# The last layer norm of a hybrid MoE step: taken without the last unit's rows, over two engines

## The chip, the cores and the metric

The kernel runs on one core of a Trainium2 chip, in one launch. The metric is the device time of that launch in microseconds (us). The kernel before took 878.97, 879.23 and 880.75 us in three runs, a median of 879.23. PE is the matrix engine, DVE the vector engine, ACT the scalar engine, POOL the general-purpose engine, which also issues the transfers of the software queue q0, and SP the engine that issues those of the hardware queue q1.

## The reference, cut to what matters

One layer over 512 prompt tokens and 64 sample tokens, 576 rows of D = 1024 float32. An input projection feeds sparse attention and a causal convolution; both are merged, projected and normed to `x1`. Then each token goes through two of 16 experts, and the second norm gives the result:

```python
h2 = x1 * (1 + sc2) + sh2
x  = layer_norm(ALPHA * x1 + (1 + g2) * hier_moe(h2, ...), ln2_g, ln2_b)
# layer_norm: (x - mean) / sqrt(var + 1e-5) * g + b, over the 1024 columns
# returns y_prompt (512 x 1024), y_sample (64 x 1024), and the new caches
```

## The kernel before, in words

Tokens lie in five tiles: four of 128 rows and one of 64. The program is written in the order of the data flow, and a scheduler of the tile framework sets each engine's own order and its waits.

**The front part.** After the conditioning vectors have been computed, three fills on POOL (L416, L418) write a constant row over and over to DRAM: one to the upper half of `z_scr`, and one for the prompt and one for the sample tokens to `h_scr`. Their sources are rows in `rows_scr`, which short POOL transfers (L412) have written just before. Then comes the input projection. For the indexer's keys, `kip` and `kis` are built on ACT and DVE, and POOL writes them out (L504). The indexer's queries come from five groups of matmuls (`tm0` to `tm4`, L144 to L146), whose results ACT copies to the tiles `st` (L514). `kis` and the `st` tiles 0, 2 and 4 share two buffers (the tag "S"), so the copy of tile 2 takes the buffer of `kis`, after `kis` has been written out.

**The MoE stage.** The scratch array `z_scr` has two halves of 576 rows, which add up to ALPHA * x1 before the experts. A token's first choice adds to its row in the lower half, its second choice to its row in the upper half. Thirteen units of work run one after the other; each takes up to 128 gathered token rows through one expert (or 64 through each of two) and ends in `add_rows`: two products on DVE (L1193), then one indirect transfer on POOL that adds the 128 rows to `z_scr` (L1194); rows that are not taken have an index out of bounds and are skipped. The last unit holds one expert. Expert weights go through a ring of 24 pieces of 128 x 1024 floats, loaded by SP.

**The end.** After the last unit, every engine reads the number of experts that had more tokens than their rows (`ovi`, L1492) and runs a loop over them, which is empty with these inputs. Then SP loads each tile's two halves of `z_scr` as one transfer (`zt`, L1525, 1 MB for a full tile). DVE adds the halves (L1527) and multiplies by the gain and adds the bias in two passes (L1529, L1530), with the mean and the root from ACT (for the first tile from DVE), and SP stores the tile to the result (L1531).

## Time and profile before

| | |
|---|---|
| runs, median | 878.97, 879.23, 880.75 us; 879.23 us |
| profiled execution | 880.75 us |
| its span on the core | 879.1 us |
| busy PE / DVE / ACT / POOL | 792.4 / 647.6 / 358.5 / 132.3 us |
| moved by q1 (SP) / q0 (POOL) | 122.74 MB / 34.26 MB |
| chain that ended last: PE / DVE / DMA / issue | 60% / 7% / 4% / 2% |

The span runs from the first to the last recorded event; the execution's own time is 1.65 us longer than it. The chain of waits is followed back from the last instruction, at each step to what released it. "DVEq", "SPq" and the like are an engine's own queue work (reading a value, issuing a transfer). In a timeline a bracket holds the idle time ahead of the instruction and what ended it.

### The profile page before, as it was taken

Reading aid. Unit: us, or ns where it says so; the run is one execution under the profiler, and the core shown is the slowest. Engines: PE = TensorE matmul, PEld = TensorE weight load, DVE = VectorE, ACT = ScalarE, POOL = GpSimd, SP = SyncE. Lnnn points to the kernel's source line nnn. Section 1 sums busy time; section 2 is a strip of 40 time slices with the busy share of each in tenths; the row PEclk is TensorE's granted clock in tenths of the full one; section 3 lists DMA queues with packets and bytes.
Section 4 is the critical chain, followed back from the end, with each engine's and each line's share of the span. In section 5 each row is a group of like instructions: output and inputs, shape, how many; then the busy total and the mean of one; then the engine's idle time right before and its main releaser. Section 6 shows DMA issues by size and latency. Waiting matters only on the chain.

```text
span 879.1 us, 13265 instructions
## 1 busy us (share of the span) xinstructions
PE 792.4 (90%) x4827; PEld 641.6 (73%) x4827; DVE 647.6 (74%) x1275; ACT 358.5 (41%) x654; POOL 132.3 (15%) x169
## 2 busy tenths in 40 slices
PE   4899999999999999999999999899938999999910
PEld 3788888887878879879899799888826676645400
DVE  1569999989999889988896425428896896655337
ACT  3243141324344335547733852312433664334304
POOL 2300000310100000000100001020347342221100
PEclk9999999999999999999999999899957999999965
DMA  9998663482423224232443106585695999699345
GB/s 295 343 340 261 195 213 119 122 241 54 149 71 95 76 75 113 89 100 84 129 118 113 39 1 228 188 259 213 197 329 139 345 366 310 199 363 373 97 164 169
DMA packets 101202, 162.06 MB, mean 184 GB/s; under 512 B 9667, under 2 KB 67163, under 8 KB 101137
## 3 DMA queue, kind: packets, MB, share of 16 engines
q1 hardware_dynamic: 87104, 122.74, 42.3%
q0 software_dynamic: 12688, 34.26, 14.5%
q10 hardware_dynamic: 1344, 4.22, 1.3%
q8 instruction: 38, 0.62, 0.3%
q14 instruction: 28, 0.22, 0.1%
HBM read 146.01 MB, written 26.13 MB: 196 GB/s over the span
## 4 chain that ended last, share of the span: by engine, by line
PE 60%; DVE 7%; DMA 4%; issue 2%; ACT 1%; POOL 1%; POOLq 0%; DVEq 0%; ACTq 0%
PE acc L242 7%; PE acc L244 7%; PE acc L243 7%; PE pd L1182 5%; PE pdot L528 3%; PE pg L1152 2%; PE pg L144 2%; DMA wraw<-in_w_att_out_dram 2%; PE pg L146 2%; PE pg L145 2%; PE tm L144 2%; PE tm L146 2%; PE tm L145 2%; PE pl L652 2%; PE po L660 2%
## 5 line engine op out<-in xcount | busy, mean ns | idle before, releaser
L588 DVE SCALAR_TENSOR_TENSOR y<-ue,dwT,y 128x604 f32<-128x604 f32 (+17 forms) x232 | 183.3, 828 | 1.9 <-ACT y L586 1.6
L242 PE MATMUL acc<-hh,wlo 128*128 128x288 f32 (+1 forms) x504 | 152.9, 304 | 1.3 <-DVE wlo L140 1.3
L243 PE MATMUL acc<-hh,whi 128*128 128x288 f32 (+1 forms) x504 | 150.6, 299 | 0.0
L244 PE MATMUL acc<-hl,whi 128*128 128x288 f32 (+1 forms) x504 | 149.4, 300 | 0.0
L139 ACT CAST whi<-wraw 128x1024 fp32r<-128x1024 f32 (+1 forms) x72 | 75.1, 1044 | 175.2 <-PE acc L244 83.1
L140 DVE TENSOR_TENSOR wlo<-wraw,whi 128x1024 fp32r<-128x1024 f32 (+1 forms) x72 | 87.4, 1214 | 53.6 <-ACT whi L139 53.3
L242 PEld LDWEIGHTS acc<-hh,wlo 128*128 128x128 f32 (+1 forms) x504 | 94.4, 187 | 17.2 <-issue 8.8
L243 PEld LDWEIGHTS acc<-hh,whi 128*128 128x128 f32 (+1 forms) x504 | 94.4, 187 | 5.2 <-issue 5.1
L244 PEld LDWEIGHTS acc<-hl,whi 128*128 128x128 f32 (+1 forms) x504 | 93.7, 187 | 5.5 <-issue 5.2
L144 PE MATMUL tm<-wlo,hh 128*128 128x512 f32 x128 | 50.5, 397 | 0.4 <-DVE wlo L140 0.4
L145 PE MATMUL tm<-whi,hh 128*128 128x512 f32 x128 | 50.4, 394 | 0.0
L146 PE MATMUL tm<-whi,hl 128*128 128x512 f32 x128 | 49.8, 391 | 0.0
L140 DVE TENSOR_TENSOR wlo<-ring,whi 128x1024 fp32r<-128x1024 f32 x30 | 36.4, 1222 | 17.7 <-ACT whi L139 15.0
L1182 PE MATMUL pd<-ring,hT 128*128 128x512 f32 x96 | 44.0, 601 | 1.2 <-ACT hT L1166 1.2
L139 ACT CAST whi<-ring 128x1024 fp32r<-128x1024 f32 x30 | 31.3, 1048 | 31.2 <-PE pg L146 27.4
L242 PE MATMUL acc<-oh,wlo 128*128 128x288 f32 x128 | 39.7, 310 | 4.5 <-DVE gt L744 4.0
L244 PE MATMUL acc<-yl,whi 128*128 128x288 f32 x128 | 39.3, 310 | 0.6 <-DVE yl L721 0.5
L244 PE MATMUL acc<-ol,whi 128*128 128x288 f32 x128 | 39.3, 310 | 0.0
L243 PE MATMUL acc<-oh,whi 128*128 128x288 f32 x128 | 39.2, 307 | 0.0
L243 PE MATMUL acc<-yh,whi 128*128 128x288 f32 x128 | 38.3, 301 | 0.0
L242 PE MATMUL acc<-yh,wlo 128*128 128x288 f32 x128 | 37.9, 297 | 0.0
L1194 POOL DMA_INDIRECT z_scr<-yo,idt x13 | 22.3, 1712 | 83.2 <-DVE yo L1193 74.4
(482 smaller groups left out, 1773.5 us busy)
## 6 DMA issues: line engine op xcount, KB each, us to landing
ring<-in_w_gate_up_dram SPq DMA_DIRECT2D x62, 512.0 KB
wraw<-in_w_in_dram SPq DMA_DIRECT2D x48, 512.0 KB
wada<-in_w_ada_dram SPq DMA_DIRECT2D x32, 512.0 KB
ring<-in_w_down_dram SPq DMA_DIRECT2D x32, 512.0 KB
wada<-in_w_ada_dram SPq DMA_DIRECT2D x32, 256.0 KB
gates_scr<-glg POOLq DMA_DIRECT2D x16, 288.0 KB
gt<-gates_scr POOLq DMA_DIRECT2D x16, 288.0 KB
wraw<-in_w_conv_out_dram SPq DMA_DIRECT2D x8, 512.0 KB
```

The lines of the kernel that those rows point to most:

```text
L139: split_copy[0] = S.copy(hi, raw).ins
L140: V.tensor_tensor(lo, raw, hi, op=OP.subtract)
L144: PE.matmul(out, lh, rl, start=start, stop=False)
L145: PE.matmul(out, lh, rh, start=False, stop=False)
L146: PE.matmul(out, ll, rh, start=False, stop=stop)
L242: PE.matmul(ps[h][0:m, 0:288], wl[:, k, :], xh[:, k, sl], start=k == 0, stop=False)
L243: PE.matmul(ps[h][0:m, 0:288], wh[:, k, :], xh[:, k, sl], start=False, stop=False)
L244: return PE.matmul(ps[h][0:m, 0:288], wh[:, k, :], xl[:, k, sl], start=False, stop=k == KT - 1).ins
L528: PE.matmul(pdt[0:n, 0:L], qiT[pr, h // 2, 128 * t:128 * t + n], kiT[pr, k0:k0 + L], start=True, stop=True)
L588: V.scalar_tensor_tensor(y[:, 30 - i:EXT], ue[:, 0:EXT - 30 + i], dwT[:, j, i:i + 1], y[:, 30 - i:EXT], op0=OP.mult, op1=OP.add)
L1182: PE.matmul(pd_[c], hT[:, k, :], dns[0][k][:, cs], start=k == 0, stop=k == 1)
L1194: sc = G.indirect_dma_start(out=z_d, out_offset=bass.IndirectOffsetOnAxis(ap=ids[1], axis=0), in_=y, in_offset=None, bounds_check=2 * T - ...
```

## The change

The result arrays are filled with the bias row `ln2_b` early, right behind the fills of `h_scr` (L421 of the changed kernel, 512 and 64 rows of 4 KB). At the end, `z_scr` is loaded into free ring pieces once the last but one unit's scatter has landed, so without what the last unit adds, and the five tiles are normed from it: DVE adds the halves and takes the sum of each row in the same pass, ACT squares and takes the root, ACT scales, DVE multiplies by the gain, and POOL adds the tile to the filled result. The last unit's tokens go apart: POOL gathers their rows of both halves of `z_scr`, DVE adds the unit's product, and this sixth tile is normed in full and written over the result by two indirect transfers (prompt rows, sample rows), behind the stores of the five tiles. The last unit's scatter to `z_scr` stays, for the overflow loop, which now has a norm of its own in its body; the loop's count is read at the very end.

```diff
--- before.py
+++ after.py
@@ -413,9 +413,12 @@
         if j >= 2:
             G.dma_start(dap(rows_d, 8 * D + c, [[D, 2], [1, 512]]), bR[32 * j:32 * j + 1, :, :])
 
-    G.dma_start(dap(z_d, T * D, [[D, T], [1, D]]), dap(rows_d, 9 * D, [[0, T], [1, D]]))
+    zero = G.dma_start(dap(z_d, T * D, [[D, T], [1, D]]), dap(rows_d, 9 * D, [[0, T], [1, D]]))
     for s, (t0, n) in enumerate(((0, SEQ), (SEQ, DEC))):
-        G.dma_start(dap(h2_d, t0 * D, [[D, n], [1, D]]), dap(rows_d, (6 + s) * D, [[0, n], [1, D]]))
+        zero = G.dma_start(dap(h2_d, t0 * D, [[D, n], [1, D]]), dap(rows_d, (6 + s) * D, [[0, n], [1, D]]))
+    with tc.issue_after(zero.ins):
+        for s, n in enumerate((SEQ, DEC)):
+            G.dma_start(dap(o["y"][s], 0, [[D, n], [1, D]]), dap(a["ln2_b"], 0, [[0, n], [1, D]]))
 
...
@@ -1272,6 +1275,16 @@
...
+    other = late.tile([128, NE], I32, name="other", bufs=1)
+    sample = late.tile([128, NE], I32, name="sample", bufs=1)
+
+    def other_rows():
+        V.scalar_tensor_tensor(tok, idt[:, 0], 2.0, idt[:, 1], op0=OP.mult, op1=OP.subtract)
+        V.tensor_scalar(other, tok, float(T), None, op0=OP.add)
+        V.tensor_scalar(tok, idt[:, 0], float(SEQ), float(OOB), op0=OP.is_lt, op1=OP.mult)
+        V.scalar_tensor_tensor(sample, idt[:, 0], -float(SEQ), tok, op0=OP.add, op1=OP.add)
+
     def static_args(es):
         e = es[0]
         w = wsl[:, e:e + 1] if e < NFIX else cols[:, 1, e - NFIX:e - NFIX + 1]
@@ -1298,6 +1311,78 @@
...
+    NR2 = NT + 1
+    st2 = late.tile([128, 4, NR2], F32, name="st2", bufs=1)
+    V.memset(st2, 1.0)
+
+    def both_rows(t):
+        return [[(16, 0), (16, 1)], [(16, 2), (16, 3)], [(17, 0), (18, 0)], [(17, 1), (18, 1)], [(17, 2), (18, 2)],
+                [(17, 3), (18, 3)]][t]
+
+    z12, last_rows = {}, [None, None]
+
+    def tile_rows(t):
+        z12[t] = [piece(*x)[0:TS[t]] for x in both_rows(t)]
+        for i, z in enumerate(z12[t]):
+            last_rows[0] = SY.dma_start(z, dap(z_d, (i * T + t * 128) * D, [[D, TS[t]], [1, D]])).ins
+
+    def z_gather(dst, idx):
+        last_rows[1] = G.indirect_dma_start(out=dst, out_offset=None, in_=z_d,
+                                            in_offset=bass.IndirectOffsetOnAxis(ap=idx, axis=0),
+                                            bounds_check=2 * T - 1, oob_is_err=False).ins
+
+    def unit_rows():
+        z12[NT] = [piece(*x) for x in both_rows(NT)]
+        z_gather(z12[NT][1], other[:, plan[-1][0]:plan[-1][0] + 1])
+        z_gather(z12[NT][0], idt[:, 1, plan[-1][0]:plan[-1][0] + 1])
+
+    def summed(t, to=None):
+        z, n = z12[t][0], z12[t][0].shape[0]
+        V.scalar_tensor_tensor(z, z, 1.0, z12[t][1] if to is None else to, op0=OP.mult, op1=OP.add,
+                               accum_out=st2[0:n, 0, t:t + 1])
+        V.tensor_scalar(st2[0:n, 0, t:t + 1], st2[0:n, 0, t:t + 1], -1.0 / D, None, op0=OP.mult)
+
+    def measured(t):
+        z, jk = z12[t]
+        n = z.shape[0]
+        S.activation(jk, z, AF.Square, bias=st2[0:n, 0, t:t + 1], accum_out=st2[0:n, 1, t:t + 1])
+
+    def rooted(t):
+        S.activation(st2[:, 2, t:t + 1], st2[:, 1, t:t + 1], AF.Sqrt, bias=epst, scale=1.0 / D)
+
+    def scaled(t):
+        V.reciprocal(st2[:, 2, t:t + 1], st2[:, 2, t:t + 1])
+        if t < NT:
+            z, n = z12[t][0], TS[t]
+            V.tensor_tensor(st2[:, 3, t:t + 1], st2[:, 0, t:t + 1], st2[:, 2, t:t + 1], op=OP.mult)
+            S.activation(z, z, AF.Identity, bias=st2[0:n, 3, t:t + 1], scale=st2[0:n, 2, t:t + 1])
+
+    rows3 = []
+
+    def rows3_loads():
+        rows3.extend(piece(16, 4 + i) for i in range(2))
+        brow(rows3[0], a["ln2_g"], 0, SY)
+        brow(rows3[1], a["ln2_b"], 0, SY)
+
+    def tile_done(t):
+        z, n = z12[t][0], TS[t]
+        V.tensor_tensor(z, z, rows3[0][0:n], op=OP.mult)
+        with tc.issue_after(last_rows[1]):
+            G.dma_start(dap(o["y"][t // 4], (t % 4) * 128 * D, [[D, n], [1, D]]), z, accum_op=OP.add)
+
+    def unit_done():
+        z, t = z12[NT][0], NT
+        V.scalar_tensor_tensor(z, z, st2[:, 0, t:t + 1], rows3[0], op0=OP.add, op1=OP.mult)
+        V.scalar_tensor_tensor(z, z, st2[:, 2, t:t + 1], rows3[1], op0=OP.mult, op1=OP.add)
+
+    def unit_store():
+        z, e = z12[NT][0], plan[-1][0]
+        for s, (idx, n) in enumerate(((idt[:, 0, e:e + 1], SEQ), (sample[:, e:e + 1], DEC))):
+            G.indirect_dma_start(out=dap(o["y"][s], 0, [[D, n], [1, D]]), out_offset=bass.IndirectOffsetOnAxis(ap=idx, axis=0),
+                                 in_=z, in_offset=None, bounds_check=n - 1, oob_is_err=False)
+
...
@@ -1380,6 +1465,14 @@
         rows_in(0)
         pend, over = [], overflow()
 
+        def do(fn, *args):
+            return lambda: fn(*args)
+
+
+        aside = {("p", len(units) - 3): [rows3_loads],
+                 ("p", len(units) - 2): [do(tile_rows, t) for t in range(2)] + [unit_rows] +
+                                        [do(tile_rows, t) for t in range(2, NT)]}
+
         def product(p):
             p.y = gate_row(p.ar[2], p.ar[3])
             p.pd = down(p.hT, p.dns)
@@ -1388,6 +1481,8 @@
                 if y.left == 0:
                     follow_down(y)
             add_rows(p.y, p.pd, p.ar[0])
+            for act in aside.pop(("p", p.u), ()):
+                act()
 
         for u, x in enumerate(units):
             if u == 2:
@@ -1399,11 +1494,12 @@
                     if len(y.es) == 2:
                         y.blocks[0] = (y.blocks[0][0], static_args(y.es))
                 token_columns(cols[:, 0, NFULL:NVAR], NFIX + NFULL, NE)
+                other_rows()
             owed[0] = int(u + 1 < len(units) and len(units[u + 1].es) == 2)
             blocks = []
             for b, _ in x.blocks:
                 p = Unit()
-                p.b, p.experts = b, x.experts
+                p.b, p.u, p.experts = b, u, x.experts
                 p.ar = dict(x.blocks)[b]
                 p.dns = [y.down for y in x.experts]
                 blocks.append(p)
@@ -1482,12 +1578,25 @@
                 step(2, q)
                 step(3, q)
             pend = blocks
-        rows3 = slot([128, 2, D], name="rows3")
-        brow(rows3[:, 0], a["ln2_g"], 0, SY)
-        brow(rows3[:, 1], a["ln2_b"], 0, SY)
-        for i in range(len(pend)):
-            turn_next(i)
-            product_next(i)
+        p = pend[0]
+        turn_next(0)
+        p.y = gate_row(p.ar[2], p.ar[3])
+        p.pd = down(p.hT, p.dns)
+        add_rows(p.y, p.pd, p.ar[0])
+        for t in range(NT + 2):
+            if t == 1:
+                V.tensor_tensor(z12[NT][0], z12[NT][0], z12[NT][1], op=OP.add)
+            if t < NR2:
+                summed(t, p.y if t == NT else None)
+                measured(t)
+            if t > 1:
+                tile_done(t - 2)
+            if t > 0:
+                scaled(t - 1)
+            if t < NR2:
+                rooted(t)
+        unit_done()
+        unit_store()
 
...
-    jk = slot([128, D], name="jk")
-
-    def act_stats(src, n):
-        mv = late.tile([128, 4], F32, name="mv", tag="mv", bufs=NT)
-        S.activation(jk[0:n], src[0:n], AF.Copy, scale=1.0 / D, accum_out=mv[0:n, 0:1])
-        V.tensor_scalar(mv[0:n, 3:4], mv[0:n, 0:1], -1.0, None, op0=OP.mult)
-        S.activation(jk[0:n], src[0:n], AF.Square, bias=mv[0:n, 3:4], accum_out=mv[0:n, 1:2])
-        S.activation(mv[0:n, 2:3], mv[0:n, 1:2], AF.Sqrt, bias=epst[0:n], scale=1.0 / D)
-        V.reciprocal(mv[0:n, 2:3], mv[0:n, 2:3])
-        return mv[0:n, 0:1], mv[0:n, 2:3]
-
-    for t in range(NT):
-        n, s = TS[t], int(t == 4)
-        z2 = slot([128, 2, D], name="zt")
-        SY.dma_start(z2[0:n], dap(z_d, t * 128 * D, [[D, n], [T * D, 2], [1, D]]))
-        zt = z2[:, 0, :]
-        V.tensor_tensor(zt[0:n], zt[0:n], z2[0:n, 1, :], op=OP.add)
-        mean, rs = stats(zt, n) if t == 0 else act_stats(zt, n)
-        V.scalar_tensor_tensor(zt[0:n], zt[0:n], mean, rows3[0:n, 0], op0=OP.subtract, op1=OP.mult)
-        V.scalar_tensor_tensor(zt[0:n], zt[0:n], rs, rows3[0:n, 1], op0=OP.mult, op1=OP.add)
-        SY.dma_start(dap(o["y"][s], (t % 4) * 128 * D, [[D, n], [1, D]]), zt[0:n])
+        ln2 = slot([128, 2, D], name="ln2")
...
```

The first place is POOL's program in the front part, between the fills and the attention's first outputs. Before:

```order
L412 DMA rows_scr<-arow 2x512 x4
L440 DMA ckt<-in_cache_k_dram 128x256
L442 DMA ckt<-in_cache_idx_k_dram 128x64 x2
L418 DMA h_scr<-rows_scr 512x1024
L418 DMA h_scr<-rows_scr 64x1024
L504 DMA out_dram<-kip 128x4x64
L504 DMA out_dram<-kis 64x64
L559 DMA out_dram<-at_1572 128x256 x3
```

And of the changed kernel:

```order
L412 DMA rows_scr<-arow 2x512 x4
L443 DMA ckt<-in_cache_k_dram 128x256
L445 DMA ckt<-in_cache_idx_k_dram 128x64 x2
L418 DMA h_scr<-rows_scr 512x1024
L418 DMA h_scr<-rows_scr 64x1024
L421 DMA out_dram<-in_ln_b_dram 512x1024
L421 DMA out_dram<-in_ln_b_dram 64x1024
L507 DMA out_dram<-kip 128x4x64
L507 DMA out_dram<-kis 64x64
L562 DMA out_dram<-at_1574 128x256 x3
```

The fill of the result, 576 rows of 4 KB, now stands ahead of the two transfers that write `kip` and `kis`; nothing else moved here.

The second place is ACT's program around the copies of the indexer's queries. Before:

```order
L514 COPY st_1825<-tm0_1684 128x512
L503 COPY kip_1653<-kip_1653 128x4x64
L514 COPY st_1839<-tm1_1685 128x512
L514 COPY st_1867<-tm3_1687 128x512
L139 CAST whi_1970<-wraw_1968 128x1024
L503 COPY kis_1654<-kis_1654 64x64
L508 COPY at2_1572<-pki_1665 128x512
L581 COPY ue_2730<-yT_587 128x512
L582 COPY ue_2730<-stT_97 128x30
...
L508 COPY at2_1572<-pki_1681 128x64
L514 COPY st_1853<-tm2_1686 128x512
L519 COPY at2_1572<-pqi_1833 128x4x128
```

And of the changed kernel:

```order
L517 COPY st_1841<-tm1_1687 128x512
L517 COPY st_1869<-tm3_1689 128x512
L506 COPY kis_1656<-kis_1656 64x64
L511 COPY at2_1574<-pki_1667 128x512
L584 COPY ue_2732<-yT_587 128x512
...
L139 CAST whi_1972<-wraw_1970 128x1024
...
L511 COPY at2_1574<-pki_1683 128x64
L517 COPY st_1855<-tm2_1688 128x512
L522 COPY at2_1574<-pqi_1835 128x4x128
```

A weight cast (`whi`) moved behind the copy of `kis`; the copy of tile 2 (`st_1853<-tm2_1686`, now `st_1855<-tm2_1688`) stays behind it and still takes the buffer that `kis` had, so in both it waits for the transfer that writes `kis` out.

The third place is the end of POOL's program, from the gather of the last unit's rows on. Before, where the last unit's scatter stands behind the overflow loop (whose body is left out):

```order
L1119 DMA xg<-h_scr,idt 128x1024
L1194 DMA z_scr<-yo,idt 1152x1024 x5
L1492 TENSOR_LOAD ovi
L1494 COMPARE_AND_BRANCH
...
L1194 DMA z_scr<-yo,idt 1152x1024
L1572 UNCONDITIONAL_BRANCH
```

And of the changed kernel, down to the loop's count (the last unit's scatter is the single one behind the first store to `out_dram`):

```order
L1122 DMA xg<-h_scr,idt 128x1024
L1197 DMA z_scr<-yo,idt 1152x1024 x5
L1332 DMA ring<-z_scr,other 128x1024
L1332 DMA ring<-z_scr,idt 128x1024
L1373 DMA out_dram<-ring 128x1024
L1197 DMA z_scr<-yo,idt 1152x1024
L1373 DMA out_dram<-ring 128x1024 x3
L1373 DMA out_dram<-ring 64x1024
L1383 DMA out_dram<-ring,idt 512x1024
L1383 DMA out_dram<-ring,sample 64x1024
L1601 TENSOR_LOAD ovi
L1603 COMPARE_AND_BRANCH
```

The five stores, which SP issued behind the loop before, are now POOL's; in the same queue stand two gathers ahead of them, the last unit's scatter behind the first of them, and two scatters behind the last. The count is read behind all of these.

## Rows read from the trace of the kernel before

**Rows 1.** Chain of waits, last 41 us: start us, us, what it waited on or did.
```profile
838.95 0.56 DVEq L1492
...
840.92 6.11 DMA z_scr<-yo,idt
847.05 5.42 DMA zt<-z_scr
852.49 1.24 DVE zt L1527
...
873.71 1.28 DVE zt L1530
```

**Rows 2.** Timeline of the last stretch: start us, us, engine, line, operation [idle before <-releaser].
```profile
830.54 1.55 POOL L1194 DMA_INDIRECT z_scr<-yo,idt  x1 [9.11 <-DVE yo L1193]
...
838.16 0.69 DVE L1193 TENSOR_TENSOR yo<-yo,pd 128x512 f32<-128x512 f32 x1 [0.63 <-PE pd L1182]
...
859.16 16.39 SPq L1531 DMA_DIRECT2D out_dram<-zt  x5
```

**Rows 3.** Windows: stretch, us, busy us (instructions) of five engines, PEclk, DMA share, GB/s.
```profile
832.50:835.50 3.00, 1.52 (x5) 0.81 (x6) 0.54 (x2) 1.80 (x3) 0.00 (x0) 1.00 0.55 75
835.50:841.00 5.50, 2.62 (x7) 0.83 (x5) 2.60 (x3) 0.89 (x1) 0.08 (x1) 1.00 0.00 0
843.00:847.00 4.00, 0.00 (x0) 0.00 (x0) 0.00 (x0) 0.00 (x0) 0.00 (x0) 0.50 0.43 64
852.50:859.20 6.70, 0.00 (x0) 0.00 (x0) 6.55 (x9) 1.45 (x3) 0.00 (x0) 0.50 1.04 414
620.30:624.70 4.40, 4.40 (x27) 3.75 (x25) 4.23 (x9) 2.32 (x4) 0.92 (x1) 1.00 0.70 112
```

**Rows 4.** Groups by shape of DVE and ACT, 839 to 879: xcount | busy us, mean ns | idle before.
```profile
L1529 DVE SCALAR_TENSOR_TENSOR zt<-zt,mv,rows 128x1024 f32<-128x1024 f32 x4 | 5.1, 1284 | 1.6 <-ACT jk L1517 1.5
...
L1527 DVE TENSOR_TENSOR zt<-zt 128x1024 f32<-128x1024 f32 x4 | 4.9, 1216 | 13.6 <-DMA zt<-z_scr 13.6
...
L1519 DVE RECIPROCAL mv<-mv 128x1 f32<-128x1 f32 x3 | 0.5, 155 | 0.0
...
L1517 ACT ACTIVATE jk<-zt,mv 128x1024 f32<-128x1024 f32 x3 | 3.4, 1148 | 1.8 <-DVE mv L1516 1.8
```

**Rows 5.** Timeline of POOL, 150 to 260.
```profile
165.73 0.67 POOL L416 DMA_DIRECT2D z_scr<-rows_scr  x1
166.58 1.01 POOL L412 DMA_DIRECT2D rows_scr<-arow  x2 [0.18 <-issue]
167.88 1.01 POOL L412 DMA_DIRECT2D rows_scr<-arow  x2 [0.29 <-DVE y L588]
...
182.19 1.15 POOL L418 DMA_DIRECT2D h_scr<-rows_scr  x2 [11.69 <-DMA rows_scr<-arow]
191.71 0.79 POOL L504 DMA_DIRECT2D out_dram<-kip  x1 [8.36 <-ACT kip L503]
196.10 0.56 POOL L504 DMA_DIRECT2D out_dram<-kis  x1 [3.60 <-issue]
218.70 0.58 POOL L559 DMA_DIRECT2D out_dram<-at  x1 [22.04 <-ACT at L552]
```

**Rows 6.** Windows around the fill of h_scr and of the convolution stage.
```profile
182.20:191.00 8.80, 8.80 (x45) 7.21 (x44) 7.43 (x15) 4.85 (x12) 1.15 (x2) 1.00 0.85 195
199.00:201.00 2.00, 1.90 (x8) 1.56 (x9) 2.00 (x3) 2.00 (x7) 0.00 (x0) 1.00 0.00 0
220.00:250.00 30.00, 30.00 (x141) 23.93 (x140) 29.90 (x62) 9.54 (x17) 4.90 (x9) 1.00 0.46 142
300.00:400.00 100.00, 100.00 (x628) 82.55 (x627) 87.70 (x199) 46.57 (x107) 5.42 (x10) 1.00 0.31 88
```

**Rows 7.** Timeline of ACT, 180 to 235.
```profile
201.29 0.58 ACT L514 COPY st<-tm 128x512 f32<-128x512 f32 x1
```

**Rows 8.** Timeline of PE, 198 to 217.
```profile
199.10 0.27 PE L507 MATMUL pki<-ident,kis 64*128 64x64 f32 x1 [0.97 <-ACT kis L503]
...
204.57 0.48 PE L144 MATMUL tm<-wlo,hh 128*128 128x512 f32 x1
...
216.02 0.50 PE L144 MATMUL tm<-wlo,hh 128*128 128x512 f32 x1 [0.43 <-DVE wlo L140]
```

More of the change, by code (lines that the diff above doesn't have):

```diff
@@ L1508, in encoder_step @@
         add_rows(y, down(turned(hidden(pg, w)), [[wt[1][:, k, :] for k in range(2)]]), ids)
-    jk = slot([128, D], name="jk")
-    def act_stats(src, n):
-        mv = late.tile([128, 4], F32, name="mv", tag="mv", bufs=NT)
-        S.activation(jk[0:n], src[0:n], AF.Copy, scale=1.0 / D, accum_out=mv[0:n, 0:1])
-        V.tensor_scalar(mv[0:n, 3:4], mv[0:n, 0:1], -1.0, None, op0=OP.mult)
-        S.activation(jk[0:n], src[0:n], AF.Square, bias=mv[0:n, 3:4], accum_out=mv[0:n, 1:2])
-        S.activation(mv[0:n, 2:3], mv[0:n, 1:2], AF.Sqrt, bias=epst[0:n], scale=1.0 / D)
-        V.reciprocal(mv[0:n, 2:3], mv[0:n, 2:3])
-        return mv[0:n, 0:1], mv[0:n, 2:3]
-    for t in range(NT):
-        n, s = TS[t], int(t == 4)
-        z2 = slot([128, 2, D], name="zt")
-        SY.dma_start(z2[0:n], dap(z_d, t * 128 * D, [[D, n], [T * D, 2], [1, D]]))
-        zt = z2[:, 0, :]
-        V.tensor_tensor(zt[0:n], zt[0:n], z2[0:n, 1, :], op=OP.add)
-        mean, rs = stats(zt, n) if t == 0 else act_stats(zt, n)
-        V.scalar_tensor_tensor(zt[0:n], zt[0:n], mean, rows3[0:n, 0], op0=OP.subtract, op1=OP.mult)
-        V.scalar_tensor_tensor(zt[0:n], zt[0:n], rs, rows3[0:n, 1], op0=OP.mult, op1=OP.add)
-        SY.dma_start(dap(o["y"][s], (t % 4) * 128 * D, [[D, n], [1, D]]), zt[0:n])
+        ln2 = slot([128, 2, D], name="ln2")
+        brow(ln2[:, 0], a["ln2_g"], 0, SY)
+        brow(ln2[:, 1], a["ln2_b"], 0, SY)
+        for t in range(NT):
+            n, s = TS[t], int(t == 4)
+            z2 = slot([128, 2, D], name="zt")
+            SY.dma_start(z2[0:n], dap(z_d, t * 128 * D, [[D, n], [T * D, 2], [1, D]]))
+            zt = z2[0:n, 0, :]
+            V.tensor_tensor(zt, zt, z2[0:n, 1, :], op=OP.add)
+            mean, rs = stats(zt, n)
+            V.scalar_tensor_tensor(zt, zt, mean, ln2[0:n, 0], op0=OP.subtract, op1=OP.mult)
+            V.scalar_tensor_tensor(zt, zt, rs, ln2[0:n, 1], op0=OP.mult, op1=OP.add)
+            SY.dma_start(dap(o["y"][s], (t % 4) * 128 * D, [[D, n], [1, D]]), zt)
 _INS = ["x_prompt", "x_sample", "cache_k", "cache_v", "cache_idx_k", "state_conv", "c_prompt", "c_sample",
```

## The prediction

> **What bounds the kernel now.** I read the chain of waits first. Most of it is PE, and only its last 41 us hold another pattern, so I read these closely [rows 1]: reading the loop's count is queued from 838.95, the last unit's scatter goes out at 840.92 and lands 6.11 later, the load of the first tile follows from 847.05 and takes 5.42, and from 852.49 DVE works through five tiles until 873.71 + 1.28 = 874.99. The reader is to see that nothing overlaps: scatter, load and norm stand end to end. The timeline adds what lies around it [rows 2]: DVE had the unit's last product done at 838.16 + 0.69 = 838.85, and the five stores are issued between 859.16 and 875.55; the span ends at 879.1, 3.55 behind. So from the last product to the end it is 40.2 us. The last but one unit's scatter is issued from 830.54 for 1.55 us.
>
> The windows show when that scatter's bytes had moved [rows 3]: traffic at 75 GB/s until 835.5, none from there to 841. Then the front part, where the change puts a fill. POOL's timeline shows what stands around it [rows 5], and the windows there say how PE does behind it [rows 6]: 30.00 busy of 30 from 220, and 100.00 of 100 from 300. A stall of PE ahead of that is not caught up. This is why a fill whose result is wanted only at the end can still cost time.
>
> **The end, part by part.** *What is removed.* The loads no longer wait for the last unit. Their condition is the scatter issued at 830.54, done by 835.5 [rows 2, 3]; with half a microsecond for SP they start at about 836.0. With the same 5.42 [rows 1] the first tile is there at 841.4 instead of 852.49, 11.1 earlier. The later tiles come faster than they are worked on: 414 GB/s in the loads' window [rows 3] is 2.5 us per tile of 1 MB. The count, some 2 us ahead of the scatter [rows 1], moves behind everything and is taken as hidden behind the last transfers, since it waits for none of them; if it isn't, it costs 2.
>
> *The new work on DVE.* A step of the new pipeline is one add with the row sums (no row of before has that form; I take the nearest, L1529's 1.284), one product with the gain (L1527's form, 1.216) and three small ones at 0.155 [rows 4]: 2.97 us. ACT's share of a step is a square (1.148 and its sum's reading) and a scaling of the same shape, some 2.6 us, so DVE paces. The whole is 1.44 for the first step, five of 2.97, 1.22 more for adding the two gathered halves of the last unit's rows, 1.4 for the last gain product (64 rows) and what is left of the small ones, 2.57 for the sixth tile's two passes: 21.5. From 841.4 that is 862.9, and with a microsecond for hand-overs between the engines at the end 863.8. So DVE ends 11.2 earlier than 874.99, although it has a tile more to norm.
>
> *The new work on POOL's queue.* Here part of it is given back. The stores were plain copies on SP's queue; now each adds to the result in memory and all stand in POOL's one queue. That this queue is served in order is seen from POOL's fills: two short transfers issued at 166.58 and 167.88, of a few KB each, release the next step only at 182.19, after the big fill issued at 165.73 ahead of them [rows 5]. A full tile's adding transfer is not in the end's rows. The nearest one is a unit's scatter of 128 valid rows in the MoE stage: 112 GB/s in its window of 4.40 us, that is 0.49 MB [rows 3], the queue's traffic being about 3.0 us of it. The last unit's scatter, about half of whose rows are valid, moved 0.26 MB in 4.0 us at 64 GB/s [rows 3], which bounds a store from above by some 3.7 us if rows and not bytes set the price; from below a store may hide wholly behind DVE's 2.97. I take 3.0, the row that is the same size. Tile 0's product is ready at about 851.3 (two steps, the square, the scaling and the product behind 841.4) and the queue starts at 851.5. The queue then holds tile 0, the unit's scatter, tiles 1 to 3 at 3.0 each and tile 4 at 1.6: 16.6 us, to 868.1, and landing is seen at 868.6. Only then may the second scatter over the result go: 1.55 for its issue [rows 2] and 3.6 until the end, as behind the last store of before: 873.8. Against 879.1 the end gains 5.3. With 3.7 per store it ends at 877.6, a gain of 1.5; with stores hidden the path is DVE's end at 863.8, 0.2, two issues of 1.55 and 3.6, that is 870.6 and a gain of 8.5.
>
> **The fill, part by part.** POOL issues it right behind the fill of `h_scr` at 182.19 [rows 5]. Both are 2.36 MB in rows of 4 KB. The window behind 182.2 shows 195 GB/s at a DMA share of 0.85, weight loads included [rows 6]; at that rate 2.36 MB is 12.1 us. Started about a microsecond after the issue, the fill of `h_scr` is done at 195.3, which agrees with `kis`, issued at 196.10 and landed by 199.0, where the window falls to 0 GB/s [rows 5, 6]. The new fill then runs from 195.3 to 207.4. `kip` and `kis` go out behind it and land at about 209.0. ACT's copy of the indexer queries' tile 2, which takes the buffer of `kis`, ran at 201.29 [rows 7]; it now ends at 209.6. ACT stands in order, so behind it wait the copies of the tiles after it and the next cast. PE wants the transposes and the next product (`tm`) of this copy at 204.57 [rows 8]; that gives a stall of 5.0. The two short waits that PE has around this place, 0.97 at 199.10 and 0.43 at 216.02 [rows 8], shrink or go in the shadow of it, about 0.6 of them: 4.4 is left. Bounds: 0, if the fill's bytes move alongside at the free 15% and faster (the fill of `h_scr` shares its window with weight loads); 6.5, if the fill also holds up the weight loads of the projection by some 2 us more.
>
> [...]
>
> *The rest.* Four tiny operations of DVE per launch, one memset, two index columns, and the earlier loads of the gain row behind unit 10 cost less than 1 us of DVE, whose idle time in the MoE stage takes it. The ring pieces used for the tiles are free then, since no weights follow. The last unit's work on PE and DVE runs beside the loads of the tiles, and SP's queue has nothing else to load then.
>
> **Sum.** -5.3 + 4.4 = -0.9 against the span of 879.1. The profiled execution is at 880.75, 1.5 over the median of the runs; the same difference applied to the median gives 879.23 - 0.9 = 878.3.
>
> **Rivals.**
> *The fill is hidden.* Then only the end counts: 879.23 - 5.3 = 873.9. For it: 15% of the DMA share is free, and the fill has no reader until the end. Against it: the queue's order [rows 5] and the measured rate [rows 6]. [...]
> *The stores don't bound, DVE does.* -8.5 + 4.4 = -4.1, so 875.1. For it: 3.0 per store and 2.97 per step are nearly the same, and one cheaper store decides it. Against it: the scatter of the last unit stands between the stores, a sixth of its own.
> *The adding stores are slow (slower than before).* One queue holds six adding transfers; at 3.7 each the end gains only 1.5 and the fill's 4.4 make +2.9: 882.1. It decides from about 3.6 per store on: there the end's gain falls below 2.6, and with 4.4 that is the bound of what counts as slower. For it: the last unit's scatter at 64 GB/s [rows 3]. Against it: the 128-row scatter at 112.
>
> **How the numbers follow.** The forecast (fill stalls PE, stores at about 3.0) has a chance of 0.45 and its own range of 878.3 +- 2.5; the hidden fill 0.15, DVE as pace 0.15, slow stores 0.25. A difference of 0.2%, 1.8 us, is what can be told from no change here. Faster by that means below 877.5: both fast rivals and a third of the forecast, 0.45. Slower means over 881.0: nearly all of the slow rival and a little of the forecast, 0.26; between them 0.29. The range reaches from 873.0, under the hidden fill, to 882.5, over the slow stores; outside remain a combination of both fast rivals and a stall of 6.5 with slow stores.
>
> **What would show it.** In the front part: POOL's issue of `kip` behind the fill, a wait of ACT at the copy of `st` near 209 put down to the transfer of `kis`, and a gap of PE of 4 to 5 us behind 204; if PE has no gap, the hidden fill holds. At the end: DVE's first add near 841 plus the stall, no wait for the last unit's scatter, DVE's last pass about 11 earlier against the last product of the unit, and behind it a queue of stores that lands 5 or more later. If the last scatter is issued within 2 us of DVE's end, DVE paces; if the stores land more than 3.6 apart, the slow rival holds. Wrong altogether would be loads that still wait for the last unit's scatter, or a PE that is slower in the MoE stage.

## The result, and the profile after

The change made the kernel slower. It took 894.25 us in the median of four runs (891.87 to 896.22) against 879.57 for the kernel before: a ratio of 1.0164, 95% interval 1.0133 to 1.0195. The prediction was 878.3 and its range ended at 882.5. The profiled execution is the shortest of the four, 891.87 us with a span of 890.2, which is 11.1 more than before.

| us in the profiled execution | before | after |
|---|---|---|
| POOL issues the first gate tile (end of the front part) | 289.70 | 296.06 |
| last product of the last unit done on DVE | 838.85 | 845.31 |
| from there to DVE's first add of a tile | 13.64 | 2.06 |
| from there to DVE's last pass | 36.14 | 29.34 |
| from there to the end of the span | 40.25 | 44.89 |

So 6.46 of the 11.1 are lost ahead of the last product, and 4.64 behind it, although the norm begins 11.6 earlier and ends 6.8 earlier there. Both places show in the profile. The mark of the front is this line of POOL, before and in the changed kernel:

```profile
289.70 0.56 POOL L710 DMA_DIRECT2D gates_scr<-glg  x1 [46.03 <-ACT rl L530]
```

```profile
296.06 0.56 POOL L713 DMA_DIRECT2D gates_scr<-glg  x1 [47.20 <-ACT rl L533]
```

**The front.** Timeline of ACT in the changed kernel, the copy that answers to [rows 7]; in the bracket the idle time ahead and what ended it:

```profile
199.39 0.19 ACT L511 COPY at<-pki 128x64 f32<-128x64 f32 x1
208.77 0.59 ACT L517 COPY st<-tm 128x512 f32<-128x512 f32 x1 [9.19 <-DMA out_dram<-kis]
```

Timeline of PE at the same place, which answers to [rows 8]:

```profile
203.76 0.39 PE L145 MATMUL tm<-whi,hh 128*128 128x512 f32 x1
209.40 0.80 PE L144 MATMUL tm<-wlo,hh 128*128 128x512 f32 x1 [5.25 <-ACT st L517]
210.00 0.63 PE L145 MATMUL tm<-whi,hh 128*128 128x512 f32 x1
```

Windows there (stretch, us, busy us of PE, PEld, DVE, ACT and POOL, granted clock, DMA share, GB/s):

```profile
204.00:209.40 5.40, 0.15 (x1) 0.00 (x0) 0.30 (x2) 0.63 (x2) 0.00 (x0) 0.88 0.59 210
209.40:214.00 4.60, 4.60 (x11) 3.64 (x12) 4.60 (x12) 0.93 (x2) 0.00 (x0) 0.50 0.01 2
214.00:218.00 4.00, 4.00 (x19) 3.00 (x18) 2.64 (x5) 2.22 (x3) 0.00 (x0) 0.89 0.01 4
```

The transfer of `kis` lands at 208.77 behind the fill (209.0 was predicted), ACT stands 9.19, and PE 5.25 (5.0 was predicted). What was not foreseen is the second line of windows: behind the idle stretch the granted clock is 0.50 until about 215. Eleven matmuls fit into 4.60 us there, one starting every 0.43 us, where from 199.00 to 203.90, at a granted clock of 1.00, a like one started every 0.23. From these starts I estimate that some 2.5 us are lost by it.

**The end.** Timeline of DVE in the changed kernel, the last product and the full-size passes from the first tile on:

```profile
844.62 0.69 DVE L1196 TENSOR_TENSOR yo<-yo,pd 128x512 f32<-128x512 f32 x1 [0.63 <-PE pd L1185]
847.37 1.23 DVE L1343 SCALAR_TENSOR_TENSOR ring<-ring 128x1024 f32<-128x1024 f32 x1 [2.06 <-DMA ring<-z_scr]
...
853.62 1.23 DVE L1588 TENSOR_TENSOR ring<-ring 128x1024 f32<-128x1024 f32 x1 [4.83 <-DMA ring<-z_scr,idt]
854.76 1.22 DVE L1343 SCALAR_TENSOR_TENSOR ring<-ring 128x1024 f32<-128x1024 f32 x1
856.36 1.23 DVE L1343 SCALAR_TENSOR_TENSOR ring<-ring 128x1024 f32<-128x1024 f32 x1
...
861.13 1.23 DVE L1343 SCALAR_TENSOR_TENSOR ring<-ring 128x1024 f32<-128x1024 f32 x1 [1.01 <-SPq L1603]
...
873.37 1.28 DVE L1378 SCALAR_TENSOR_TENSOR ring<-ring,st 128x1024 f32<-128x1024 f32 x1
```

Timeline of POOL there, the second gather, then the stores and scatters that answer to the stores of [rows 2]:

```profile
844.45 1.03 POOL L1332 DMA_INDIRECT ring<-z_scr,idt  x1 [0.30 <-issue]
860.15 0.98 POOL L1373 DMA_DIRECT2D out_dram<-ring  x1 [14.67 <-DVE st L1359]
863.87 1.61 POOL L1197 DMA_INDIRECT z_scr<-yo,idt  x1 [2.74 <-SPq L1603]
864.92 1.54 POOL L1373 DMA_DIRECT2D out_dram<-ring  x1
866.78 0.89 POOL L1373 DMA_DIRECT2D out_dram<-ring  x1 [0.32 <-DVE st L1359]
869.59 0.85 POOL L1373 DMA_DIRECT2D out_dram<-ring  x1 [1.92 <-DVE st L1359]
872.37 0.86 POOL L1373 DMA_DIRECT2D out_dram<-ring  x1 [1.93 <-DVE ring L1371]
879.97 1.07 POOL L1383 DMA_INDIRECT out_dram<-ring,idt  x1 [6.74 <-DMA out_dram<-ring]
881.35 1.02 POOL L1383 DMA_INDIRECT out_dram<-ring,sample  x1 [0.30 <-issue]
```

Windows over loads and stores, which answer to [rows 3]:

```profile
844.00:854.00 10.00, 0.58 (x2) 0.00 (x0) 2.45 (x5) 2.82 (x4) 1.18 (x2) 0.79 1.02 395
855.00:861.00 6.00, 0.00 (x0) 0.00 (x0) 4.14 (x11) 4.54 (x7) 0.85 (x1) 0.50 0.72 126
872.00:878.00 6.00, 0.00 (x0) 0.00 (x0) 2.62 (x4) 0.00 (x0) 0.86 (x1) 0.50 1.04 195
884.00:890.00 6.00, 0.00 (x0) 0.00 (x0) 0.00 (x0) 0.00 (x0) 0.00 (x0) 0.50 0.00 1
```

The first tile is there when it was forecast, 2.06 behind the last product. But DVE then waits 4.83 for the two gathers, and 1.01 more ahead of the fourth tile's sum ("SPq L1603" is SP's queue at the loop; what DVE needs is a tile, so the landing of its load is the likelier cause). The loads move 395 GB/s up to 854 and only 126 from 855 to 861, where the first store is issued only at 860.15. The second store stands 4.77 behind the first, since the last unit's scatter, ahead of it in the queue, goes out only at 863.87; in e3 below, which has no loop, the bracket of this scatter names the loads of `z_scr`. The last two stores go out 2.8 apart, as DVE delivers, but at 195 GB/s the queue still has work when the last is issued, and the two scatters over the result wait 6.74 for it. Their bytes have moved by 883.6, and next to nothing moves in the more than 6 us from there to the end of the span.

### The profile page after: what moved, and what is told of

Read it like the earlier page. It is cut to its first block, busy times and chain, and to the rows that moved or that the text cites. A ratio compares the mean times of both kernels' runs of the same rounds, so it can differ in the third digit from the quotient of the medians.

```text
span 890.2 us, 13322 instructions
## 1 busy us (share of the span) xinstructions
PE 794.7 (89%) x4827; PEld 642.7 (72%) x4827; DVE 647.1 (73%) x1290; ACT 362.2 (41%) x656; POOL 142.0 (16%) x180
## 4 chain that ended last, share of the span: by engine, by line
PE 73%; DMA 13%; DVE 7%; issue 4%; ACT 1%; POOL 1%; POOLq 0%; SPq 0%; DVEq 0%; ACTq 0%
PE acc L242 11%; PE acc L244 10%; PE acc L243 10%; PE pd L1185 4%; DMA wraw<-in_w_in_dram 3%; PE pdot L531 3%; DMA out_dram<-ring 2%; PE pg L1155 2%; PE tm L144 2%; PE tm L146 2%; PE tm L145 2%; PE pg L144 2%; PE pl L655 2%; PE po L663 2%; DMA wraw<-in_w_att_out_dram 2%
## 5 line engine op out<-in xcount | busy, mean ns | idle before, releaser
L591 DVE SCALAR_TENSOR_TENSOR y<-ue,dwT,y 128x600 f32<-128x600 f32 (+27 forms) x232 | 182.9, 828 | 1.9 <-ACT y L589 1.5
L713 POOL DMA_DIRECT2D gates_scr<-glg x16 | 8.7, 544 | 174.4 <-ACT glg L712 104.9
```

Of the source, the lines that this page charges most:

```text
L591: V.scalar_tensor_tensor(y[:, 30 - i:EXT], ue[:, 0:EXT - 30 + i], dwT[:, j, i:i + 1], y[:, 30 - i:EXT], op0=OP.mult, op1=OP.add)
```

## The experiments

Twelve kernels ran. The stretch from the first gate tile to the last product, which no experiment's edit touches, takes between 545.4 and 551.5 us in the fourteen profiles: it shifts by several us from one execution to the next. The kernel before, run beside each group of experiments, had medians from 878.15 to 880.35, so differences between medians of two groups can be off by some 2. So beside medians I read two marks in each profile: when POOL issues the first gate tile, and the stretch from the last product to the end (the tail). The tails of the changed kernel and of the two kernels that have the same tail code, e1 and e5, are 44.9, 45.3 and 47.0: a difference of 2 in one tail is at the edge of what a profile can tell. DVE's last pass ends 29.3, 28.9 and 31.1 behind the last product in these three, so it has the same spread.

| kernel | median us (runs) | ratio to before, 95% | first gate tile | tail |
|---|---|---|---|---|
| before | 879.57 (4), 878.15 to 880.35 in later groups | | 289.70 | 40.25 |
| changed | 894.25 (4) | 1.0133 to 1.0195 | 296.06 | 44.9 |
| e1 fill behind kis | 885.28 (7) | 1.0048 to 1.0100 | 290.80 | 45.3 |
| e2 late add | 894.40 (4) | 1.0141 to 1.0212 | 298.43 | 45.5 |
| e3 no loop | 893.45 (4) | 1.0122 to 1.0176 | 298.06 | 43.4 |
| e4 before + fill | 889.08 (4) | 1.0083 to 1.0150 | 298.44 | 40.25 |
| e5 kis by ACT's queue | 884.54 (10) | 1.0048 to 1.0102 | 288.76 | 47.0 |
| e6 scatter behind | 889.31 (4) | 1.0067 to 1.0206 | 296.70 | 42.8 |
| e7 plain stores | 889.91 (4) | 1.0053 to 1.0187 | 296.88 | 40.7 |
| e8 wide load | 894.36 (1) | | 298.36 | 43.1 |
| e9 plain, bias on POOL | 896.82 (6) | 1.0158 to 1.0223 | 289.90 | 54.5 |
| e10 e5 + e6 + e8 | 882.76 (12) | 1.0012 to 1.0054 | 289.01 | 43.3 |
| e11 e2 + e8 | 891.99 (4) | 1.0096 to 1.0166 | 297.84 | 41.3 |
| e12 e10 + e2 | 884.19 (12) | 1.0020 to 1.0072 | 288.86 | 41.9 |

**e1, the fill behind the two short transfers**

```diff
-    with tc.issue_after(zero.ins):            # behind the fills of h_scr
-        for s, n in enumerate((SEQ, DEC)):
-            G.dma_start(dap(o["y"][s], 0, ...), dap(a["ln2_b"], 0, ...))
...
-        G.dma_start(dap(o["idx_k"][t0 // 4], 0, ...), kv[0:n, :, 0:64])
+        zero = G.dma_start(dap(o["idx_k"][t0 // 4], 0, ...), kv[0:n, :, 0:64])
...
+    with tc.issue_after(zero.ins):            # behind the transfer of kis
+        for s, n in enumerate((SEQ, DEC)):
+            G.dma_start(dap(o["y"][s], 0, ...), dap(a["ln2_b"], 0, ...))
```

> The changed kernel with one edit: the fill of the result is issued behind the two short transfers that write kip and kis, not ahead of them. PE's order then is that of the kernel before. Theory (the fill delays kis, the copy of tile 2 waits, PE stands 5.25 us and then runs some 5 us at the lower clock): 6.4 faster than the changed kernel, about 888, no wait of ACT for kis. Rival (the fill's bytes or the other order of PE cost the time): no more than 2 faster, 892 or above.

885.28, 9.0 less than the changed kernel, or 8.5 if each is set against the kernel before of its own group. PE's longest wait between 196 and 260 is 0.85; the first gate tile goes out at 290.80. The theory's 6.4 was too small: it was read from the execution with the shortest stall of all profiles with the fill in that place (5.25; e4 below has the longer ones).

**e4, the fill alone**

```diff
 # the kernel before, with the fill of the changed one
+    with tc.issue_after(zero.ins):            # zero: the last fill of h_scr
+        for s, n in enumerate((SEQ, DEC)):
+            G.dma_start(dap(o["y"][s], 0, ...), dap(a["ln2_b"], 0, ...))
```

> The kernel before with one edit: the fill of the result where the changed kernel has it (later overwritten by the plain stores). Theory (the front costs 6.4): 886.0 against 879.5. Rival (part of the delay up to the last unit comes from the loads and index columns of the new end): under 884.

889.08, 9.9 more than the 879.14 of before beside it, and its tail is before's, 40.25. The fill by itself thus costs about two thirds of the whole loss. Wait of PE between 190 and 230 in e4 (waiter, what for, us in total, times, longest):

```profile
PE tm L144 <- ACT st L517: 7.2, 1, 7.2
```

In the changed kernel's profile the same row reads 5.3; in the other kernels that have the fill in this place PE stands 6.3 to 7.8. A stall of 7.2 and some 2.5 for the low clock behind it, less the two short waits of before (1.4) that go, are 8.3; the first gate tile is 8.7 late.

**e5, kis by ACT's queue: the fill's order or its bytes?**

```diff
-        G.dma_start(dap(o["idx_k"][t0 // 4], 0, ...), kv[0:n, :, 0:64])
+        (G if t0 == 0 else S).dma_start(dap(o["idx_k"][t0 // 4], 0, ...), kv[0:n, :, 0:64])
```

> The changed kernel with one edit: kis is written out by ACT's own queue, so it doesn't stand behind the fill; the fill stays where it is, and PE's order stays that of the changed kernel but for five instructions. Theory (queue order makes the stall of 5 to 8 us, and the lower clock behind it 2 to 3 more): no wait of ACT for kis, no fall of the clock, 7 to 9 faster than the changed kernel, 885 to 887. Rival (the fill's bytes or the other order of PE cost the time): no more than 2 faster.

884.54, 9.7 less. Here the fill stands where the changed kernel has it and PE's order is the changed kernel's but for five instructions; only 16 KB have left the queue. Timeline of ACT and windows of e5:

```profile
203.76 0.59 ACT L517 COPY st<-tm 128x512 f32<-128x512 f32 x1 [3.06 <-DMA out_dram<-kis]
```

```profile
204.00:209.40 5.40, 5.00 (x24) 3.94 (x25) 5.40 (x13) 2.26 (x5) 0.00 (x0) 1.00 0.84 242
209.40:214.00 4.60, 4.60 (x24) 3.72 (x23) 4.60 (x10) 2.25 (x3) 0.00 (x0) 1.00 0.15 17
```

PE is busy beside 242 GB/s of traffic, the clock stays at 1.00, 24 matmuls run in the window that held 11, and the first gate tile goes out at 288.76, 0.9 ahead of the kernel before. So neither the fill's bytes nor the other order of the matmuls cost a time that these runs can tell: the loss was the place of one small transfer behind a big one in a queue.

**e2, the late add of the gathered halves**

```diff
-            if t == 1:
+            if t == NT:
                 V.tensor_tensor(z12[NT][0], z12[NT][0], z12[NT][1], op=OP.add)
```

> The changed kernel with one edit: DVE adds the two gathered halves of the last unit's rows just ahead of that tile's own sum, not behind the first tile. Theory (DVE stood 4.83 us for the gathers and all stores came later by it): DVE's last pass and the last store about 4.5 earlier, 889.8. Rival (the stores' queue on POOL bounds, so DVE's wait was hidden): within 1 of the changed kernel, 893.5.

894.40, no change. It is the rival's number, but not by the rival's mechanism. Timeline of DVE in e2:

```profile
849.46 1.23 DVE L1343 SCALAR_TENSOR_TENSOR ring<-ring 128x1024 f32<-128x1024 f32 x1 [2.48 <-DMA ring<-z_scr]
854.20 1.23 DVE L1343 SCALAR_TENSOR_TENSOR ring<-ring 128x1024 f32<-128x1024 f32 x1 [3.31 <-SPq L1603]
857.59 1.23 DVE L1343 SCALAR_TENSOR_TENSOR ring<-ring 128x1024 f32<-128x1024 f32 x1 [1.70 <-SPq L1603]
...
862.97 1.23 DVE L1343 SCALAR_TENSOR_TENSOR ring<-ring 128x1024 f32<-128x1024 f32 x1 [2.55 <-SPq L1603]
```

The wait of 4.83 is gone and others stand in its place. The fourth sum starts 16.0 behind the last product, in the changed kernel 15.8: the loads were late whatever DVE did. The rival that I had put against it (DVE earlier, POOL's queue as the bound) was not the reason either, since DVE's last pass ends 30.7 behind the last product, no earlier than the changed kernel's 29.3.

**e8 and e11, the wide load of the narrow tile**

```diff
 # as e11 has it; e8 loads the same rows and norms the first 64 of them
-            last_rows[0] = SY.dma_start(z, dap(z_d, (i * T + t * 128) * D, [[D, TS[t]], [1, D]])).ins
+            first = i * T + (t * 128 if t < 4 else T - 128)     # the last 128 rows, all partitions
+            last_rows[0] = SY.dma_start(z, dap(z_d, first * D, [[D, 128], [1, D]])).ins
```

> The changed kernel with one edit: the tile of 64 rows is loaded as 128 rows, the last 128 of each half, onto all partitions (left out: the norm of the sample rows, whose place other rows take). Theory (the loads' slow end, 0.14 MB per us where they moved 0.4, comes from the transfer to 64 partitions): twice the bytes, but the loads' end within 1 us of the changed kernel's or earlier. Rival (the slow end has another cause, or bytes alone count): the end 1.5 to 4 later.

Windows of e8 over the loads:

```profile
850.00:861.00 11.00, 0.00 (x0) 0.00 (x0) 4.07 (x10) 2.98 (x5) 0.00 (x0) 0.56 1.02 402
861.00:865.00 4.00, 0.00 (x0) 0.00 (x0) 3.10 (x8) 3.76 (x7) 0.23 (x1) 0.50 0.47 186
```

The loads move 0.5 MB more, and are over about 15.5 behind the last product where they were over 16.6 behind it. So the slow end of the changed kernel comes at least in part from loading the last tile into 64 partitions. The last stretch moves 126 GB/s with that tile, behind 395, and 186 without it, behind 402. By what means the narrow tile slows the loads was not shown, and why e8's last stretch is slower than the rest stays open.

> The changed kernel with the late add of the gathered halves (which alone moved nothing) and the 64-row tile loaded as 128 rows with the last 64 stored. Same result. Theory (the wait for the gathers and the late landing of the fourth tile cover each other, so that either alone leaves DVE's end where it was): DVE's last pass 2 to 4 earlier against the last product than in the changed kernel (29.3 behind it), the stretch from the last product to the end 41 to 42 in place of 44.9. Rival (the wait for the gathers never mattered): as with the wide load alone, DVE's end 28.7 behind the last product, the stretch 43.

With both edits the tail is 41.3, 3.6 less than the changed kernel's and in the theory's 41 to 42; the late add alone had given nothing and the wide load 1.8. DVE, however, ends 28.2 behind the last product, which is nearer to the rival's 28.7 than to the theory's 25.3 to 27.3. Timeline of DVE in e11, the fourth sum now 13.4 behind the last product:

```profile
862.73 1.23 DVE L1344 SCALAR_TENSOR_TENSOR ring<-ring 128x1024 f32<-128x1024 f32 x1
```

It started 15.1 behind with the wide load alone, but the gathers' add then still has to be done behind it, so that the sixth tile's sum starts 20.3 behind the last product, for 20.7. That the two waits covered each other is pointed to by the tail and by where the waits went in e2; it is not shown, as the gain over e8 is within the spread of the tails.

**e6, the last unit's scatter behind the stores**

```diff
-        add_rows(p.y, p.pd, p.ar[0])          # products and scatter
+        for c in range(2):                    # the products alone
+            cs = slice(512 * c, 512 * c + 512)
+            V.tensor_tensor(p.y[:, cs], p.y[:, cs], p.pd[c], op=OP.mult)
...
         unit_done()
+        with tc.issue_after(stores[-1]):      # stores: the five tile stores
+            add_only(p.y, p.ar[0])            # the scatter alone
         unit_store()
```

> The changed kernel with one edit: the last unit's scatter to z_scr goes out behind the five tile stores, not between the first and the second. Theory (this scatter waits for the last tile's load, which lands only some 20 us after the loads start, and holds the stores behind it in POOL's queue): store of tile 1 issued 1 us after its product, the stores' landing 2 to 3 earlier, 891.5. Rival (the queue's bytes at 0.2 MB per us bound it wherever the scatter stands): within 1 of 894.

889.31, and a tail of 42.8, 2.1 less. POOL in e6:

```profile
858.89 0.99 POOL L1378 DMA_DIRECT2D out_dram<-ring  x1 [14.23 <-DVE st L1362]
862.87 0.91 POOL L1378 DMA_DIRECT2D out_dram<-ring  x1 [2.99 <-DVE st L1362]
...
875.34 1.03 POOL L1388 DMA_INDIRECT out_dram<-ring,idt  x1 [0.31 <-issue]
```

The second store follows the first by 4.0, in the changed kernel by 4.8, and the scatter over the result goes 31.1 behind the last product, where it went 34.7. From there to the end it is 11.8 in place of 10.2, with the moved scatter now right ahead of it in the queue, and so 3.6 earlier become 2.1. The size is near what one profile can tell, and the interval of the ratio overlaps the changed kernel's: pointed to, not proven.

**e7, plain stores**

```diff
-            G.dma_start(dap(o["y"][t // 4], ...), z, accum_op=OP.add)
+            G.dma_start(dap(o["y"][t // 4], ...), z)
```

> The changed kernel with one edit: the five tile stores are plain, they don't add (left out: the bias of the rows that are not the last unit's). Theory (an adding store moves 0.2 MB per us where SP's plain loads moved 0.4): with plain stores the backlog of 5 us behind the last store's issue falls to about 2.5, and the time by 3 to 5: 890. Rival (the price is POOL's queue, not the adding): within 1 of 894.

889.91 and a tail of 40.7, 4.2 less. POOL in e7:

```profile
874.81 0.55 POOL L1373 DMA_DIRECT2D out_dram<-ring  x1 [2.25 <-DVE ring L1371]
878.55 1.04 POOL L1383 DMA_INDIRECT out_dram<-ring,idt  x1 [3.19 <-DMA out_dram<-ring]
```

The wait for the stores' landing is 3.19 in place of 6.74, in the same queue, and the scatter goes 30.4 behind the last product for 34.7. From 872 to 874 the plain stores move 348 GB/s at a DMA share of 1.01, where the adding ones moved 195 at 1.04 from 872 to 878. So the trace shows the adding as the price, and not POOL's queue. It is the largest change of the tail by any one edit here; the interval of the ratio still overlaps the changed kernel's.

**e3, no loop at the end**

```diff
-    nvals = nc.values_load_multi_w_load_instructions(ovi[...], ...)[1]
-    with tc.For_i(0, nvals[0], 1) as i:
-        ...
```

> The changed kernel without the overflow loop and the reading of its count at the end (left out: the work for experts with more tokens than rows, of which there is none with these inputs). Theory (the count is read only after the last scatter has landed, so it stands in the path): 4 to 5 us between landing and end go, 889.8. Rival (the 7.8 us behind the last issue are the scatter's landing): within 1, 893.5.

893.45 and a tail of 43.4, 1.5 less. The median is the rival's 893.5, but the trace is not the rival's: from the first scatter over the result to the end it is 7.6, where it is 10.2 to 10.4 in the changed kernel and in e1, e2, e5, e7, e8 and e11. So the loop costs about 2.6 and not 4 to 5; the front of this execution (298.06) and its wait for the stores (7.44) hide it in the time. The last bytes have moved by 889.0, 3.9 ahead of the end; in the changed kernel it is 6.6, before 1.7. What the 3.9 are made of stays open; the profile puts 2.4 of them to SP waiting for PE's queue at the program's last line, in the changed kernel 4.3.

**e9, e10 and e12, versions with the same result**

```diff
 # e9: no fill; wide load; last scatter behind everything
+        G.tensor_tensor(z, z, rows3[1], op=OP.add)
+        SY.dma_start(dap(o["y"][t // 4], ...), z[128 - n:128])
-        G.dma_start(dap(o["y"][t // 4], ...), z, accum_op=OP.add)
```

> The changed kernel without the fill: POOL adds the bias row to each normed tile in SBUF and SP stores the tiles plainly; the last unit's scatter stands behind everything on POOL; the tile of 64 rows is loaded as the last 128 rows, of which the last 64 are stored. Same result as the changed kernel. Theory (the front's delay is the fill's alone; at the end the adding stores cost 4, the scatter between them 2, the narrow load 1.5 to 2): no delay in the front, the stretch from the last product to the end 45 - 7 or 8 + 1 to 2 for POOL's add = 38 to 40 against 40.2 of the kernel before, so 877 to 879, about level with it. Rival (POOL's add of a tile takes over 3 us or slows DVE): 882 or above.

896.82, the rival's side: the tail is 54.5. Timelines of DVE and then of POOL in e9:

```profile
864.68 0.15 DVE L1357 RECIPROCAL st<-st 128x1 f32<-128x1 f32 x1
864.87 2.33 DVE L1360 TENSOR_TENSOR st<-st 128x1 f32<-128x1 f32 x1
```

```profile
864.84 2.34 POOL L1375 TENSOR_TENSOR ring<-ring 128x1024 f32<-128x1024 f32 x1 [2.63 <-DVE st L1357]
```

A product of 128x1, 0.16 us in the changed kernel, takes 2.33, just as long as POOL's add beside it; it is so at the first four tiles, and at the fifth a pass of DVE takes 3.24 in place of 1.28. The product ends at 867.20, as POOL's add does at 867.18; the reciprocal ahead of it (0.15) ended before POOL's add began, at 864.84. So the product is slow where it runs beside the add; by what means was not shown. DVE's last pass ends 39.0 behind the last product. There is no delay in front, with the first gate tile at 289.90: that half of the theory held.

> The changed kernel with three edits together, each tried by itself: kis by ACT's queue, the last unit's scatter behind the tile stores, the 64-row tile loaded as 128 rows with the last 64 stored. Same result. Theory (the three are separate terms): 894.3 - 9.5 - 2 - 1.5 to 2 = 881, still not faster than the kernel before, since the adding stores stay. Rival (they overlap at the end): 884 or above.

882.76 against 881 expected: the front's term goes whole, of the 3.5 to 4 at the end about 1.6 come (tail 43.3), so the terms of the end do not add up. Still 0.12% to 0.54% slower than before.

> The changed kernel with kis by ACT's queue, the last unit's scatter behind the tile stores, the wide load and the late add. Same result. Theory (the late add now counts): 1 to 3 faster than without it (882.8), 880 to 882, within 0.2% of the kernel before. Rival (POOL's adding stores bound the end, so that DVE's gain is given back there): 882.8, as without it.

884.19, no gain over e10 in the medians, though DVE ends 28.4 behind the last product in place of 29.2 and the tail is 41.9 in place of 43.3. So the theory's 1 to 3 did not come, and the rival, that the adding stores give DVE's gain back, is not ruled out. No version here beats the kernel before.

## Why the prediction was wrong

- *The mechanism in front was right, its price was not.* Queue order, the landing of `kis`, the copy that waits and PE's stall came as worked out (208.77 for 209.0, 5.25 for 5.0), and e1, e4 and e5 show that it is this: moved behind the two transfers (e1), the fill leaves the first gate tile about 1 late; put into the kernel before by itself (e4), it brings the whole loss of the front; left in place with `kis` on another queue (e5), it brings none. The step that failed is "4.4 is left": it left out the low clock behind the stall. In the profiled execution the stall of 5.25 plus some 2.5 for the clock, less the two waits that went (1.4), is 6.4. In the seven other profiles with the fill in this place the stall is 6.3 to 7.8 and the first gate tile 7.0 to 8.7 late; by the medians of e1, e4 and e5 the front costs 8 to 10. The bound of 6.5 was therefore no bound. That the stall of the profiled execution came so near the forecast is in part luck: it is the shortest of the eight.
- *The rival of the hidden fill* is refuted by the landing at 208.77 and PE's stall of 5.25; the rate of the row, 195 GB/s, was nearly the right one (POOL's queue moved 4.79 MB in the 26 us from 183 to 209).
- *The start of the norm was right* (2.06 behind the last product, 2.55 forecast). The step that failed is "the later tiles come faster than they are worked on". It took 414 GB/s from a stretch of 1 MB transfers over 128 partitions, and left out two gathers beside them and the 64-row tile. No row of mine was of that tile alone, but the trace of before held a sign: right behind the window of [rows 3], from 859.2 to 861, it moves 146 GB/s at a DMA share of 1.07, with half a MB of the loads left, the size of that tile, and the first store just issued. DVE ended 29.3 behind the last product, 25.0 were forecast: 4.4 later.
- *The stores.* 3.0 us each was about right: 195 GB/s is 2.7 per full tile, and 167 GB/s, the mean from 866 to 878.3, is 3.1. But the first store went out 14.8 behind the last product (12.7 forecast), for DVE was late; the last unit's scatter went 18.6 behind it (15.7 forecast), and from there to the stores' landing it was 16.1 (14.1 forecast). So the queue's end came 34.7 behind the last product and not 29.8. The rival "DVE paces" was wrong: DVE ends at 29.3, and the queue lets the scatters go 5.3 later. The slow rival had the right direction, but its 3.7 per store is not seen; its 882.1 was too low because it, too, had the front at 4.4 and the last step at 5.2.
- *The last step*, "1.55 for its issue and 3.6 until the end", failed: both scatters stand behind the wait (2.4 for the two issues), not the second alone, and the count, "taken as hidden", comes behind their landing. From the wait to the end it is 10.2 and not 5.2: 5 more. Of these the loop is 2.6 (e3), where 2 had been put to it if it isn't hidden; what the rest behind the last bytes is stays open.
- The sum: 2.1 in front, 4.9 until the stores have landed and 5.1 behind are about 12, which is the way from 878.2 to the span of 890.2. The median lies another 2.4 above this execution, whose stall is the shortest seen, while the forecast had been set 1.5 below the profiled execution of before: together they are the 15.9 between 878.3 and 894.25.

## What to carry to other kernels

A transfer that nobody waits for still stands in a queue (here `kis` landed 13.2 us after its issue, behind the fill): before a big fill is put there, look up which small transfers come behind it and whose buffers they free, and price a stall of PE with the slower clock that followed it here (0.50 for about 5 us behind 5.25). Work that is pulled forward ends when its last input lands, so read the rate of the narrowest and latest transfer, not of the widest (here 126 GB/s, not 395). An edit that removes a wait and changes nothing has not shown that the wait was free: look in its trace at where the wait went, as in e2, where the tiles' loads took its place.

## What the runs showed of the hardware

- The last stretch of the loads, with a tile of 64 partitions, moved 126 GB/s behind a stretch at 395 (changed kernel); with 128 rows in its place it moved 186 behind 402 (e8), and the loads ended sooner (15.5 for 16.6 behind the last product) with 0.5 MB more.
- Adding stores on POOL's queue moved 195 GB/s at a DMA share of 1.04 (changed kernel, 872 to 878), plain ones in the same queue 348 at 1.01 (e7, 872 to 874); the wait behind them was 3.19 for 6.74.
- 16 KB in POOL's queue behind a fill of 2.36 MB landed 13.2 us after their issue (195.55 to 208.77, changed kernel); PE stood 5.25 us for them.
- After PE had stood 5.25 us the granted clock was 0.50 for about 5 us (changed kernel), which cost some 2.5 us, an estimate from the 0.43 us between two starts of matmuls in place of 0.23.
- While POOL added a bias tile to a tile of 128x1024 (2.34 us, e9), a product of 128x1 on DVE took 2.33 in place of the changed kernel's 0.16.
